# Seven products in every quad of gate and up, with two low parts a block made by an accumulating DMA

## The chip, the core and the metric

The kernel runs on one core of a Trainium2 chip. The metric is the time of one execution on the device in microseconds (us), lower is better. The engines that matter are TensorE (PE, with its weight loads as PEld), VectorE (DVE), ScalarE (ACT), GpSimd (POOL) and SyncE (SP, which issues the loads). Each works through its own list of instructions in a fixed order; semaphores let one wait for another.

## The reference

The block is a mixer (sparse attention beside a state-space branch), a SwiGLU channel mixer and a final norm, on 256 tokens with 2048 features, all in float32. The change touches the channel mixer:

```python
u2 = rms_norm(h, g_ffn[i])
gate, up = jnp.split(u2 @ w_ffn_in[i], 2, axis=-1)
h = h + (jax.nn.silu(gate) * up) @ w_ffn_out[i]
return rms_norm(h, g_final)
```

`w_ffn_in` is 2048 x 11264 (gate and up, 5632 each), `w_ffn_out` is 5632 x 2048.

## The kernel before

**Three matmuls a product.** TensorE multiplies a rounded format (float32r). Every float32 operand is split in a high part, `hi` (a rounding copy, by ACT), and a low part, `lo` = operand - `hi` (by DVE), and a product is hi x hi + hi x lo + lo x hi: three matmuls of 128 x 512. A weight block is 1 MB (128 x 2048), loaded by SP into a buffer `raw` (three of them, pool `wraw`). `hi` and `lo` are tiles of 128 x 1024; four pairs of them are in `whi`/`wlo` and every fifth pair comes from the pool `xtra` (`hl_tiles`, line 148), so five pairs are in flight.

**Gate and up.** The 11264 columns are taken as 11 pairs (`pair`, line 829) of 512 gate and 512 up columns. A pair goes through K = 2048 in four quads of 512, each of two blocks (`block7`, line 788), here called (quad, part): (0,0), (0,1), (1,0) ... (3,1). Tokens are two tiles of 128, columns two of 512, K slices two: a 2 x 2 x 2 product of matrices for the first block and the first half of the quad. Where `QUADS[q]` is 1, block (q,0) takes Strassen's seven products (Winograd's form) in place of eight, and needs sums of weight slices first: `ta` and `tb` (lines 747 to 749, three DVE instructions), and then hi and lo of seven 512-column operands in place of four. Block (q,1), and both blocks of a quad with 0, take the eight products of the common form. The sums go to seven banks of PSUM, `ps[1]` to `ps[7]`, over the whole pair. `QUADS = (1, 1, 1, 0)`: 3 x (7 + 8) + 16 = 61 products, 183 matmuls a pair.

After a pair come its closing steps: seven adds on DVE from PSUM (line 834), two Silu on ACT, two multiplications on DVE, eight transposes on PE (line 225) and their split in hi and lo, which gives the tile `act`.

**The order.** Nothing is ordered by hand; a list scheduler puts each engine's instructions in the order in which they would be ready, by priority. `tc.high_priority(PRE)` draws loads and splits ahead, and the closing adds have twice that.

**Down.** `gemm` (line 154) multiplies the `act` tiles of a group of pairs with `w_f2`, four column blocks `nb` of 512, and DVE adds each result into `h_sb` (line 869). There were two groups, pairs 0 to 4 and pairs 5 to 10 (`SPLIT_PAIRS = 5`). In the last group, `late=16` holds back the second token tile's last 16 K slices, so that the first tile's closing steps run beside them.

**Buffers.** The pool `big` has 11 tiles of 8 KB a partition. In gate and up it holds `h_sb` (2), `opa` (4, the operands of the quads), one `act` a pair and `gf`. The pool `smx` is closed before `xtra` is opened in its place.

Of the kernel before, what the change touches and what calls it, by code (L numbers as in the profile page):

```python
# [8 lines left out]
F32 = mybir.dt.float32  # L9
F32R = mybir.dt.float32r  # L10
# [4 lines left out]
P = 128  # L15
# [12 lines left out]
SH = 64  # L28
# [4 lines left out]
NEG_VIS = -3.0e38  # L33
NEG_SEL = -3.4028e38
NEG_BIAS = -1.0e30
SPLIT_PAIRS = 5

QUADS = (1, 1, 1, 0)


C_GM = 0
# [21 lines left out]
def hybrid_block(ctx, tc, xt, x, consts, cols, heads, gfin, w_a, w_i, w_m, w_g, w_ab, w_sb, w_o, w_f1, w_f2, out):  # L63
# [79 lines left out]
        return r  # L143

    xtra = []
    turn = [0]

    def hl_tiles():
        turn[0] += 1
# [114 lines left out]
    lhs_u = lhs_of(u_hi, u_lo)  # L264


    wz = cp.tile([P, 512], mybir.dt.bfloat16, name="wz")
    nc.vector.memset(wz, 0.0)
    for i in range(9):
        warm = sd_t([P, 512], name="warm")  # L270
# [30 lines left out]
    def rs(t):  # L301
        return rstd[:, t : t + 1]

    rope = cp.tile([P, 384], F32, name="rope")
    for t in range(T):
        for base, dst, w in ((K_CA, 0, 64), (K_SA, 128, 64), (K_CI, 256, 32), (K_SI, 320, 32)):
            nc.vector.tensor_scalar_mul(rope[:, dst + t * w : dst + (t + 1) * w], tabs[:, base - K_T + t * w : base - K_T + (t + 1) * w], rs(t))
# [18 lines left out]
        nc.vector.tensor_tensor(dv[:, :, 0, :], dv[:, :, 0, :], tv[:, :, 0, :], ALU.subtract)  # L326
        nc.vector.tensor_tensor(dv[:, :, 1, :], dv[:, :, 1, :], tv[:, :, 1, :], ALU.add)

    widx = cp.tile([P, T, NIDX], F32, name="widx")
    wk0 = mid_t([P, 1024], name="wk0")  # L330
    wk1 = mid_t([P, 1024], name="wk1")
    kdup = wk0[:, 0:256].rearrange("p (t n) -> p t n", t=T)
# [36 lines left out]
    tp = tr_t([P, 5, SH])  # L369
    for i, src in enumerate((r1[:, 0:P], r1[:, P:S], dl[:, 0:P], dl[:, P:S], rest)):  # L370
        nc.tensor.transpose(tp[:, i, :], src, ident[:SH, :SH])
    dcols = cp.tile([P, 5, SH], F32, name="dcols")
    nc.vector.tensor_copy(dcols, tp)


# [8 lines left out]
    kbd_l = mid_t([P, 2, S], F32R, name="kbdl")  # L384
    split(kbd_h, kbd_l, kbd)

    isc = [cp.tile([P, P * (t + 1)], F32, name=f"isc{t}") for t in range(T)]
    inits = [tabs[:, K_V0 - K_T : K_V0 - K_T + P], tabs[:, K_V1 - K_T : K_V1 - K_T + S]]
    seen = [False] * T

# [328 lines left out]

        return get  # L720

    def halves(raw, cuts):

        out = {}
        for i, n in cuts:
            hi, lo = (v[:, : n * 512] for v in hl_tiles())
            src = raw[:, i : i + n, :].rearrange("p k n -> p (k n)")
            nc.scalar.activation(hi, src, AF.Copy)  # L728
            nc.vector.tensor_tensor(lo, src, hi.bitcast(F32), ALU.subtract)  # L729
            for j in range(n):  # L730
                out[i + j] = hi[:, j * 512 : (j + 1) * 512], lo[:, j * 512 : (j + 1) * 512]
        return out

    nts = [0]

    def fetch(w, i, seven):

        with tc.high_priority(PRE):
            raw = wraw.tile([P, 4, 512], F32, tag="raw", name=nm("raw"))
            nc.sync.dma_start(raw.rearrange("p k n -> p (k n)"), w[i])  # L740
            if not seven:
                return halves(raw, ((0, 2), (2, 2)))
            b = halves(raw, ((0, 2),))
            nts[0] += 1
            ta = mid_t([P, 2, 512], name="ta")
            tb = mid_t([P, 2, 512], name="tb") if nts[0] % 2 else xtra[0].tile([P, 2, 512], F32, tag="tb", name=nm("tb"))
            nc.vector.tensor_tensor(ta, raw[:, 2:4, :], raw[:, 1:3, :], ALU.subtract)  # L747
            nc.vector.tensor_tensor(tb[:, 0, :], raw[:, 3, :], ta[:, 0, :], ALU.subtract)  # L748
            b["last"] = nc.vector.tensor_tensor(tb[:, 1, :], raw[:, 0, :], tb[:, 0, :], ALU.subtract)
            for base, t in ((6, tb), (4, ta)):  # L750
                for j, v in halves(t, ((0, 2),)).items():
                    b[base + j] = v
            b.update(halves(raw, ((3, 1),)))
            return b
# [7 lines left out]
    for nb in range(4):  # L762
        xr = ev_t([P, T, 512], "xr")
        for t in range(T):
            nc.gpsimd.dma_start(xr[:, t, :], x[t * P : (t + 1) * P, nb * 512 : (nb + 1) * 512])
        ps = gemm(w_o, 4 * nb, 512, KT, lhs_m)
        if nb == 3:
            ahead = fetch(w_f1, 0, QUADS[0])
        for t in range(T):
            a = h_sb[t][:, nb * 512 : (nb + 1) * 512]  # L770
            with tc.issue_after(ahead["last"].ins) if nb == 3 else nullcontext():
                nc.vector.tensor_tensor(a, ps[t], xr[:, t, :], ALU.add)
            nc.scalar.activation(xr[:, t, :], a, AF.Square, accum_out=sq4[:, t, nb : nb + 1])
        ops.append(quad_ops(nb))
# [6 lines left out]
    pctx.close()  # L781
    mm = ctx.enter_context(tc.tile_pool(name="mmf", bufs=7, space=bass.MemoryType.PSUM, reuse_waits="tile"))
    trp = ctx.enter_context(tc.tile_pool(name="trf", bufs=1, space=bass.MemoryType.PSUM, reuse_waits="tile"))
    gf = big_t([P, D], name="gf")
    sq5 = sm.tile([P, T, 5], F32, tag="sq5", bufs=1, name="sq5")
    acts = []

    def block7(w, first, quads, get, ahead=None):

        n7 = sum(quads)
        n1 = 4 * len(quads) - 2 * n7
        left = {i: 3 * n7 for i in (1, 6, 7)}
        left.update({i: 3 * (n7 + n1) for i in (2, 3, 4, 5)})
        ps = {}

        def prod(i, a, b):
            start = i not in ps
            if start:  # L800
                ps[i] = mm.tile([P, 512], F32, tag="mm", name=nm(f"p{i}"))
            for j, (x, y) in enumerate(((a[0], b[0]), (a[0], b[1]), (a[1], b[0]))):
                left[i] -= 1
                nc.tensor.matmul(ps[i], x, y, start=start and j == 0, stop=left[i] == 0)  # L804

        for q, seven in enumerate(quads):
            for part in range(2):
                if q == part == 0 and ahead is not None:
                    b = ahead
                else:  # L810
                    b = fetch(w, first + 2 * q + part, seven and part == 0)
                if seven and part == 0:
                    prod(1, get(q, 0), b[1])
                    prod(2, get(q, 2), b[0])
                    prod(6, get(q, 9), b[6])
                    prod(4, get(q, 3), b[7])
# [12 lines left out]
    def pair(p):  # L829
        ps = block7(w_f1, 8 * p, QUADS, lambda q, i: ops[q](i), ahead if p == 0 else None)  # L830
        xa, xb = ev_t([P, T, 512], "xa"), ev_t([P, T, 512], "xb")
        x1, x2, x3, x4 = xa[:, 0, :], xa[:, 1, :], xb[:, 0, :], xb[:, 1, :]
        r0, r1 = rstd2[:, 0:1], rstd2[:, 1:2]
        add = lambda o, i, b: nc.vector.tensor_tensor(o, ps[i], b, ALU.add)
        with tc.high_priority(2 * PRE):
            nc.scalar.activation(x1, ps[1], AF.Copy)
            add(x2, 6, x1)
            add(x3, 7, x2)
            add(x1, 2, x1)
            nc.scalar.activation(x1, x1, AF.Silu, scale=r0)  # L840
# [12 lines left out]
    for p0, p1 in ((0, SPLIT_PAIRS), (SPLIT_PAIRS, NPAIR)):
        acts = [pair(p) for p in range(p0, p1)]
        if p0 == 0:
            nc.gpsimd.dma_start(gf, gfin.partition_broadcast(P))
        else:
            hg = [big_t([P, D], name="hg") for _ in range(T)]
        lhs_a = lhs_quads(acts)
        for nb in range(4):  # L860
            ps = gemm(w_f2, first, 512, 4 * (p1 - p0), lhs_a, late=16 if p0 > 0 and nb == 3 else 0)
            first += p1 - p0
            last = p0 > 0 and nb == 3
            for t in range(T):
# [24 lines left out]
def _layout(inp):  # L889
# [56 lines left out]
    def pack7(n0, n1, quads):  # L946
# [32 lines left out]
```

## Time and profile before

| | before |
|---|---|
| median of 3 runs | 1976.47 us (1976.05 to 1976.49) |
| profiled execution | 1976.07 us |
| its span | 1974.1 us |
| gate and up, pairs 0 to 4 | 1256.6 to 1469.6 us |
| down, first group | 1469.6 to 1579.4 us |
| gate and up, pairs 5 to 10 | 1579.4 to 1833.3 us |
| down, second group, until the last matmul | 1833.3 to about 1965 us |
| loads, all queues | 375.7 MB, 190 GB/s |

Busy time says how much of the span an engine worked; whether it sets the time is read from what it waits for. Starts of neighbouring matmuls tell the pace of PE, since their durations overlap. A row of a group gives line, engine, operation, out<-in, its count, then busy time in us, mean ns of one, and the idle time of the engine before it with what ended it.

### The profile page before, as it was taken

Reading aid. Unit: us, or ns where it says so; the run is one execution under the profiler, and the core shown is the slowest. Engines: PE = TensorE matmul, PEld = TensorE weight load, DVE = VectorE, ACT = ScalarE, POOL = GpSimd, SP = SyncE. Lnnn points to the kernel's source line nnn. Section 1 sums busy time; section 2 is a strip of 40 time slices with the busy share of each in tenths; the row PEclk is TensorE's granted clock in tenths of the full one; section 3 lists DMA queues with packets and bytes.
Section 4 is the critical chain, followed back from the end, with each engine's and each line's share of the span. In section 5 each row is a group of like instructions: output and inputs, shape, how many; then the busy total and the mean of one; then the engine's idle time right before and its main releaser. Section 6 shows DMA issues by size and latency. Waiting matters only on the chain. (4 is left out here: it accounts for less than half of the span.)

```text
span 1974.1 us, 23523 instructions
## 1 busy us (share of the span) xinstructions
PE 1961.1 (99%) x9131; PEld 1626.0 (82%) x9131; DVE 1424.0 (72%) x1918; ACT 1040.2 (53%) x1249; POOL 36.2 (2%) x87
## 2 busy tenths in 40 slices
PE   9999999999999999999999999999999999999998
PEld 7898888888888888888888888788888888888886
DVE  7898867778778756566654556788975589888644
ACT  6575564654555544555554445655553355565443
POOL 0000000000000000000000000000000000000000
PEclk9999999999999999999999999999999999999999
DMA  7645555554554555544555556465565555556553
GB/s 279 229 153 183 184 200 178 192 194 169 204 202 157 185 184 182 189 171 163 190 181 192 192 184 203 164 212 197 179 226 192 192 193 210 194 199 222 188 196 113
DMA packets 54431, 375.70 MB, mean 190 GB/s; under 512 B 6304, under 2 KB 6816, under 8 KB 10672
## 3 DMA queue, kind: packets, MB, share of 16 engines
q1 hardware_dynamic: 51120, 360.86, 52.2%
q0 software_dynamic: 1968, 11.60, 1.7%
q8 instruction: 71, 1.16, 0.2%
q10 hardware_dynamic: 1232, 1.75, 0.2%
q14 instruction: 40, 0.33, 0.1%
HBM read 372.02 MB, written 2.16 MB: 190 GB/s over the span
## 5 line engine op out<-in xcount | busy, mean ns | idle before, releaser
L195 DVE TENSOR_TENSOR lo<-raw,hi 128x1024 fp32r<-128x1024 f32 (+2 forms) x513 | 619.1, 1209 | 394.2 <-ACT hi L194 392.3
L194 ACT ACTIVATE hi<-raw 128x1024 fp32r<-128x1024 f32 (+2 forms) x513 | 536.7, 1048 | 626.4 <-PE mm L165 555.5
L164 PE MATMUL mm<-lo,uh 128*128 128x512 f32 (+2 forms) x1184 | 461.0, 389 | 0.0
L165 PE MATMUL mm<-hi,ul 128*128 128x512 f32 (+2 forms) x1184 | 458.2, 388 | 0.2 <-DVE ul L216 0.2
L163 PE MATMUL mm<-hi,uh 128*128 128x512 f32 (+2 forms) x1184 | 453.0, 389 | 1.2 <-ACT hi L194 1.2
L804 PE MATMUL p<-hi,opa 128*128 128x512 f32 x924 | 308.2, 390 | 0.0
L163 PEld LDWEIGHTS mm<-hi,uh 128*128 128x128 f32 x1184 | 222.4, 188 | 44.9 <-ACT hi L194 2.1
L165 PEld LDWEIGHTS mm<-hi,ul 128*128 128x128 f32 x1184 | 222.6, 188 | 42.5 <-DVE ul L216 0.5
L164 PEld LDWEIGHTS mm<-lo,uh 128*128 128x128 f32 x1184 | 222.7, 188 | 41.1 <-issue 0.3
L728 ACT ACTIVATE hi<-raw 128x1024 fp32r<-128x1024 f32 (+1 forms) x176 | 169.6, 978 | 118.1 <-PE p L804 101.2
L729 DVE TENSOR_TENSOR lo<-raw,hi 128x1024 fp32r<-128x1024 f32 (+1 forms) x176 | 194.6, 1119 | 27.7 <-ACT hi L728 27.0
L804 PEld LDWEIGHTS p<-hi,opa 128*128 128x128 f32 x924 | 173.5, 188 | 36.0
L804 PE MATMUL p<-lo,opa 128*128 128x512 f32 x462 | 180.2, 390 | 0.4 <-DVE lo L729 0.4
L163 PE MATMUL mm<-hi,act 128*128 128x512 f32 x352 | 137.2, 390 | 0.0
L164 PE MATMUL mm<-lo,act 128*128 128x512 f32 x352 | 137.2, 390 | 0.0
L165 PE MATMUL mm<-hi,act 128*128 128x512 f32 x352 | 137.0, 389 | 0.0
L804 PE MATMUL p<-hi,opb 128*128 128x512 f32 x352 | 130.5, 392 | 0.8 <-ACT opf L693 0.8
L804 PEld LDWEIGHTS p<-lo,opa 128*128 128x128 f32 x462 | 86.8, 188 | 18.6 <-DVE lo L729 0.9
L165 PE MATMUL mm<-hi,yl 128*128 128x512 f32 x256 | 100.4, 392 | 0.0
L164 PE MATMUL mm<-lo,yh 128*128 128x512 f32 x256 | 100.4, 392 | 0.0
L163 PE MATMUL mm<-hi,yh 128*128 128x512 f32 x256 | 100.2, 395 | 0.0
L804 PEld LDWEIGHTS p<-hi,opb 128*128 128x128 f32 x352 | 66.1, 188 | 14.5 <-ACT opf L693 1.3
(260 smaller groups left out, 2314.3 us busy)
## 6 DMA issues: line engine op xcount, KB each, us to landing
raw<-in_w_f_dram SPq DMA_DIRECT2D x132, 1024.0 KB, 4.8
raw<-in_w_m_dram SPq DMA_DIRECT2D x104, 1024.0 KB, 4.8
raw<-in_w_sb_dram SPq DMA_DIRECT2D x32, 1024.0 KB, 4.8
raw<-in_w_g_dram SPq DMA_DIRECT2D x32, 1024.0 KB, 4.8
raw<-in_w_ab_dram SPq DMA_DIRECT2D x16, 1024.0 KB, 4.8
raw<-in_w_o_dram SPq DMA_DIRECT2D x16, 1024.0 KB, 4.8
abc<-acum_d POOLq DMA_DIRECT2D x8, 1024.0 KB, 5.2
raw<-in_w_i_dram SPq DMA_DIRECT2D x8, 768.0 KB, 4.4
```

The costliest lines, as they stand in the source:

```text
L163: nc.tensor.matmul(o, lh, rh, start=(kt == 0), stop=False)
L164: nc.tensor.matmul(o, lh, rl, start=False, stop=False)
L165: nc.tensor.matmul(o, ll, rh, start=False, stop=(kt == nk - 1))
L194: hi_ops.append(nc.scalar.activation(hi[:, o], src[:, o], AF.Copy))
L195: nc.vector.tensor_tensor(lo[:, o], src[:, o], hi[:, o].bitcast(F32), ALU.subtract)
L728: nc.scalar.activation(hi, src, AF.Copy)
L729: nc.vector.tensor_tensor(lo, src, hi.bitcast(F32), ALU.subtract)
L804: nc.tensor.matmul(ps[i], x, y, start=start and j == 0, stop=left[i] == 0)
```

## The change

- `QUADS = (1, 1, 1, 1)`: quad 3 takes seven products too. A pair is 60 products, 180 matmuls. `w_f1` is packed to match, on the host.
- In pairs 1 to 10 block (0,1) is fetched ahead, in the middle of the pair before (`early`, called when block (3,0) has been fetched). Its two low parts are not made by DVE: ACT writes `lo` = -`hi` (a copy with scale -1), POOL issues a DMA that adds `raw` to `lo` in SBUF (512 KB each, two a block), and ACT writes `hi`. These tiles, `dhi` and `dlo`, come from `big`.
- A fourth buffer `raw`, in `xtra`, for every fourth fetch: these are the blocks (1,1) and the (0,1) that are made by DMA. Small tiles move from `cp` to `smx` and `mid` to make room.
- The down projection runs in four groups, pairs 0-1, 2-4, 5-7 and 8-10, so that at most three `act` tiles are held; `gf` is loaded at the last group. `h` is added to 32 times in place of 16. `late` is 12, all K slices of the last group.

```diff
-SPLIT_PAIRS = 5
-
-QUADS = (1, 1, 1, 0)
+PAIR_GROUPS = ((0, 2), (2, 5), (5, 8), (8, 11))
+
+QUADS = (1, 1, 1, 1)
...
-    wz = cp.tile([P, 512], mybir.dt.bfloat16, name="wz")
+    wz = mid_t([P, 512], mybir.dt.bfloat16, name="wz")
...
-    rope = cp.tile([P, 384], F32, name="rope")
+    rope = smx.tile([P, 384], F32, tag="rope", bufs=1, name="rope")
...
-    def halves(raw, cuts):
+    def halves(raw, cuts, by_dma=False):
+
 
         out = {}
-        for i, n in cuts:
-            hi, lo = (v[:, : n * 512] for v in hl_tiles())
+        if by_dma:
+            his, los = big_t([P, 2, 1024], F32R, name="dhi"), big_t([P, 2, 1024], F32R, name="dlo")
+        for c, (i, n) in enumerate(cuts):
             src = raw[:, i : i + n, :].rearrange("p k n -> p (k n)")
-            nc.scalar.activation(hi, src, AF.Copy)
-            nc.vector.tensor_tensor(lo, src, hi.bitcast(F32), ALU.subtract)
+            if by_dma:
+                hi, lo = his[:, c, :], los[:, c, :]
+                nc.scalar.activation(lo, src, AF.Copy, scale=-1.0)
+                nc.gpsimd.dma_start(lo, src, accum_op=ALU.add)
+                nc.scalar.activation(hi, src, AF.Copy)
+            else:
+                hi, lo = (v[:, : n * 512] for v in hl_tiles())
+                nc.scalar.activation(hi, src, AF.Copy)
+                nc.vector.tensor_tensor(lo, src, hi.bitcast(F32), ALU.subtract)
...
-    def fetch(w, i, seven):
+    ahead = {}
+
+    def fetch(w, i, seven, by_dma=False):
 
         with tc.high_priority(PRE):
-            raw = wraw.tile([P, 4, 512], F32, tag="raw", name=nm("raw"))
+            turn[1] += 1
+            raw = (xtra[0] if turn[1] % 4 == 0 else wraw).tile([P, 4, 512], F32, tag="raw", name=nm("raw"))
             nc.sync.dma_start(raw.rearrange("p k n -> p (k n)"), w[i])
             if not seven:
-                return halves(raw, ((0, 2), (2, 2)))
+                return halves(raw, ((0, 2), (2, 2)), by_dma)
...
-                if q == part == 0 and ahead is not None:
-                    b = ahead
-                else:
-                    b = fetch(w, first + 2 * q + part, seven and part == 0)
+                b = ahead.pop((q, part), None) or fetch(w, first + 2 * q + part, seven and part == 0)
+                if q == len(quads) - 1 and part == 0:
+                    early()
...
+        def early():
+            if p + 1 < NPAIR:
+                ahead[0, 1] = fetch(w_f1, 8 * p + 9, False, True)
...
-    for p0, p1 in ((0, SPLIT_PAIRS), (SPLIT_PAIRS, NPAIR)):
+    for p0, p1 in PAIR_GROUPS:
+        end = p1 == NPAIR
         acts = [pair(p) for p in range(p0, p1)]
...
-            ps = gemm(w_f2, first, 512, 4 * (p1 - p0), lhs_a, late=16 if p0 > 0 and nb == 3 else 0)
+            ps = gemm(w_f2, first, 512, 4 * (p1 - p0), lhs_a, late=12 if end and nb == 3 else 0)
```

**Where instructions move, first place: the loads at the border of two pairs, on SP.** Before, at the border of pairs 2 and 3, the loads stand in the order of their blocks: (2,1), (3,0), (3,1) of pair 2, then (0,0), (0,1), (1,0) of pair 3.

```order
L740 DMA raw_10875<-in_w_f_dram 128x2048
L740 DMA raw_10909<-in_w_f_dram 128x2048
L740 DMA raw_10943<-in_w_f_dram 128x2048
L740 DMA raw_11006<-in_w_f_dram 128x2048
L740 DMA raw_11057<-in_w_f_dram 128x2048
L740 DMA raw_11091<-in_w_f_dram 128x2048
```

Now, on SP at the border of pairs 3 and 4: (2,1), (3,0), then (0,1) of the next pair (11593), (3,1), then (1,1) of the next pair (11806), and only then (0,0) (11687) and (1,0) (11762).

```order
L751 DMA raw_11536<-in_w_f_dram 128x2048
L751 DMA raw_11570<-in_w_f_dram 128x2048
L751 DMA raw_11593<-in_w_f_dram 128x2048
L751 DMA raw_11624<-in_w_f_dram 128x2048
L751 DMA raw_11806<-in_w_f_dram 128x2048
L751 DMA raw_11687<-in_w_f_dram 128x2048
L751 DMA raw_11762<-in_w_f_dram 128x2048
```

What moved: 11593 and 11806 share the fourth buffer, so 11806 waits until both accumulating DMAs have read 11593, and (0,0) of the next pair stands behind it. Three of the six borders inside groups have this order; at the other three (0,0) stands ahead of that load. On ACT, in the same place, the negations (`dlo`) stand between the hi of blocks (2,0) (11492), (2,1) and (3,0):

```order
L737 ACTIVATE hi_11511<-raw_11492 128x512
L732 ACTIVATE dlo_11596<-raw_11593 128x1024
L734 ACTIVATE dhi_11595<-raw_11593 128x1024
L737 ACTIVATE hi_11538<-raw_11536 128x1024
L732 ACTIVATE dlo_11596<-raw_11593 128x1024
L734 ACTIVATE dhi_11595<-raw_11593 128x1024
L212 ACTIVATE act_11324<-tr_11332 128x512
L737 ACTIVATE hi_11572<-raw_11570 128x1024
```

The second negation stands right behind the hi of the first tile of (2,1); before, nothing stood there but the hi of the next tiles.

**Second place: PE where the first group of pairs ends and its down projection begins.** Before (after pair 4, `act_10653` is the tile of pair 1, `act_11667`, not yet here, that of pair 4), the transposes of the last pair stand among matmuls of earlier pairs, 63 of which follow before the first that reads `act_11667`:

```order
L163 MATMUL mm_11684<-hi_11721,act_10653 128x512
L225 MATMUL tr_11668<-kc,xa_11653 128x128
L225 MATMUL tr_11668<-kc,xb_11654 128x128
L225 MATMUL tr_11668<-kc,xa_11653 128x128
L225 MATMUL tr_11668<-kc,xb_11654 128x128
L164 MATMUL mm_11684<-lo_11722,act_10653 128x512
L165 MATMUL mm_11684<-hi_11721,act_10653 128x512
```

Now (after pair 1, `act_10340` is the tile of pair 0 and `act_10688` that of pair 1) all matmuls on pair 0 for two column blocks, 48 of them, come first, and the first matmul on `act_10688` stands right behind the four transposes that it is made from:

```order
L165 MATMUL mm_10776<-hi_10795,act_10340 128x512
L225 MATMUL tr_10689<-kc,xa_10674 128x128
L225 MATMUL tr_10689<-kc,xb_10675 128x128
L225 MATMUL tr_10689<-kc,xa_10674 128x128
L225 MATMUL tr_10689<-kc,xb_10675 128x128
L163 MATMUL mm_10703<-hi_10741,act_10688 128x512
L164 MATMUL mm_10703<-lo_10742,act_10688 128x512
L163 MATMUL mm_10704<-hi_10741,act_10688 128x512
```

At the other three such places 22 or more matmuls stand between.

More of the change, by code (lines that the diff above doesn't have):

```diff
@@ L145, in hybrid_block @@
     xtra = []
-    turn = [0]
+    turn = [0, 0]
     def hl_tiles():
@@ L327, in rope_apply @@
         nc.vector.tensor_tensor(dv[:, :, 1, :], dv[:, :, 1, :], tv[:, :, 1, :], ALU.add)
-    widx = cp.tile([P, T, NIDX], F32, name="widx")
+    widx = smx.tile([P, T, NIDX], F32, tag="widx", bufs=1, name="widx")
     wk0 = mid_t([P, 1024], name="wk0")
@@ L371, in hybrid_block @@
         nc.tensor.transpose(tp[:, i, :], src, ident[:SH, :SH])
-    dcols = cp.tile([P, 5, SH], F32, name="dcols")
+    dcols = smx.tile([P, 5, SH], F32, tag="dcols", bufs=1, name="dcols")
     nc.vector.tensor_copy(dcols, tp)
@@ L385, in hybrid_block @@
     split(kbd_h, kbd_l, kbd)
-    isc = [cp.tile([P, P * (t + 1)], F32, name=f"isc{t}") for t in range(T)]
+    isc = [smx.tile([P, P * (t + 1)], F32, tag=f"isc{t}", bufs=1, name=f"isc{t}") for t in range(T)]
     inits = [tabs[:, K_V0 - K_T : K_V0 - K_T + P], tabs[:, K_V1 - K_T : K_V1 - K_T + S]]
@@ L767, in hybrid_block @@
         if nb == 3:
-            ahead = fetch(w_f1, 0, QUADS[0])
+            ahead[0, 0] = fetch(w_f1, 0, QUADS[0])
         for t in range(T):
             a = h_sb[t][:, nb * 512 : (nb + 1) * 512]
-            with tc.issue_after(ahead["last"].ins) if nb == 3 else nullcontext():
+            with tc.issue_after(ahead[0, 0]["last"].ins) if nb == 3 else nullcontext():
                 nc.vector.tensor_tensor(a, ps[t], xr[:, t, :], ALU.add)
@@ L783, in hybrid_block, with block7 @@
     trp = ctx.enter_context(tc.tile_pool(name="trf", bufs=1, space=bass.MemoryType.PSUM, reuse_waits="tile"))
-    gf = big_t([P, D], name="gf")
     sq5 = sm.tile([P, T, 5], F32, tag="sq5", bufs=1, name="sq5")
     acts = []
-    def block7(w, first, quads, get, ahead=None):
+    def block7(w, first, quads, get, ahead, early):
         n7 = sum(quads)
@@ L829, in pair @@
     def pair(p):
-        ps = block7(w_f1, 8 * p, QUADS, lambda q, i: ops[q](i), ahead if p == 0 else None)
+        def early():
+            if p + 1 < NPAIR:
+                ahead[0, 1] = fetch(w_f1, 8 * p + 9, False, True)
+        ps = block7(w_f1, 8 * p, QUADS, lambda q, i: ops[q](i), ahead, early)
         xa, xb = ev_t([P, T, 512], "xa"), ev_t([P, T, 512], "xb")
@@ L852, in hybrid_block @@
     first = 0
-    for p0, p1 in ((0, SPLIT_PAIRS), (SPLIT_PAIRS, NPAIR)):
+    for p0, p1 in PAIR_GROUPS:
+        end = p1 == NPAIR
         acts = [pair(p) for p in range(p0, p1)]
-        if p0 == 0:
+        if end:
+            gf = big_t([P, D], name="gf")
             nc.gpsimd.dma_start(gf, gfin.partition_broadcast(P))
-        else:
             hg = [big_t([P, D], name="hg") for _ in range(T)]
@@ L860, in hybrid_block @@
         for nb in range(4):
-            ps = gemm(w_f2, first, 512, 4 * (p1 - p0), lhs_a, late=16 if p0 > 0 and nb == 3 else 0)
+            ps = gemm(w_f2, first, 512, 4 * (p1 - p0), lhs_a, late=12 if end and nb == 3 else 0)
             first += p1 - p0
-            last = p0 > 0 and nb == 3
+            last = end and nb == 3
             for t in range(T):
@@ L869, in hybrid_block @@
                     nc.vector.tensor_tensor(a, ps[t][:, c * n : (c + 1) * n], a, ALU.add)
-                    if p0 > 0:
+                    if end:
                         jk = ev_t([P, 1024], "jk")[:, :n]
@@ L956, in _layout @@
         pack7(wf1[:, 512 * p : 512 * (p + 1)], wf1[:, DFF + 512 * p : DFF + 512 * (p + 1)], QUADS) for p in range(NPAIR)])
-    cut = SPLIT_PAIRS * 512
-    a["w_f2"] = np.concatenate([pack(wf2, (s, s + 512), k0, k1) for k0, k1 in ((0, cut), (cut, DFF)) for s in range(0, D, 512)])
+    a["w_f2"] = np.concatenate([pack(wf2, (s, s + 512), 512 * p0, 512 * p1) for p0, p1 in PAIR_GROUPS for s in range(0, D, 512)])
     return a
```

## The prediction, made before the changed kernel ran

> **What bounds the kernel now.** First the engine totals of the page, then what PE waits for in the whole run.
>
> ```profile
> PE 1961.1 (99%) x9131; PEld 1626.0 (82%) x9131; DVE 1424.0 (72%) x1918; ACT 1040.2 (53%) x1249; POOL 36.2 (2%) x87
> ...
> PE p L804 <- ACT opf L693: 0.8, 1, 0.8
> PE p L804 <- DVE lo L729: 0.4, 1, 0.4
> ```
>
> PE is busy for 99% of the span, and the channel mixer's two rows in its list of waits come to 1.2 us. So nothing that other engines save can help there, and a matmul that goes shortens the run by its pace, as long as no new wait opens. The pace comes from the timeline of PE in gate and up (start, duration): the first two and the last of 24 matmuls in a row.
>
> ```profile
> 1650.70 0.39 PE L804 MATMUL p<-hi,opb 128*128 128x512 f32 x1
> 1650.93 0.39 PE L804 MATMUL p<-lo,opa 128*128 128x512 f32 x1
> ...
> 1655.91 0.39 PE L804 MATMUL p<-hi,opa 128*128 128x512 f32 x1
> ```
>
> 23 steps in 5.21 us are 0.2265 us a matmul; the 0.39 is a pipelined duration and not the cost. Next, how near the other engines are, by stretches: one whole pair, and the sum of three (columns: stretch, length, then busy us of PE, PEld, DVE, ACT, POOL, granted clock, DMA share, GB/s); then the opening of gate and up, and the first down projection.
>
> ```profile
> 1658.84:1701.32 42.48, 42.48 (x192) 35.14 (x191) 36.98 (x43) 24.31 (x28) 0.00 (x0) 1.00 0.58 198
> ...
> sum 127.42, PE 127.42 PEld 105.41 DVE 112.27 ACT 72.83 POOL 0.00; mean PE 42.47 PEld 35.14 DVE 37.42 ACT 24.28 POOL 0.00
> ...
> 1256.60:1469.60 213.00, 211.72 (x948) 174.58 (x947) 184.73 (x206) 123.79 (x143) 2.08 (x6) 1.00 0.57 199
> 1469.60:1579.40 109.80, 109.80 (x489) 90.89 (x489) 61.67 (x60) 43.84 (x43) 0.61 (x1) 1.00 0.55 195
> ```
>
> A pair takes 42.47 us, all of it PE; DVE works for 37.42 (88%) and ACT for 24.28. In down DVE is at 56%. The granted clock is 1.00 throughout, so it is no term here. DVE is the engine that could take PE's place.
>
> **The change part by part.** *Removed on PE.* 61 products become 60, three matmuls a pair, 33 in all: 33 x 0.2265 = **7.5 us**. All of it is on the path, since PE waits for nothing. A pair is then 42.47 - 0.68 = 41.8 us.
>
> *DVE in gate and up.* Its cost is read from starts, which follow each other back to back:
>
> ```profile
> 1638.72 1.22 DVE L729 TENSOR_TENSOR lo<-tb,hi 128x1024 fp32r<-128x1024 f32 x1
> 1639.86 1.22 DVE L729 TENSOR_TENSOR lo<-ta,hi 128x1024 fp32r<-128x1024 f32 x1
> 1640.99 0.69 DVE L729 TENSOR_TENSOR lo<-raw,hi 128x512 fp32r<-128x512 f32 x1
> 1641.59 0.68 DVE L213 TENSOR_TENSOR act<-tr,act 128x512 fp32r<-128x512 f32 x1
> ```
>
> 1.13 us for 1024 elements, 0.60 for 512. A block of seven products costs ta 1.13, tb 2 x 0.60 and low parts 3 x 1.13 + 0.60 = 6.3 us, a common one 2 x 1.13 = 2.3. So quad 3 adds 4.1, and the block made by DMA takes 2.3 away: +1.8 us, 39.2 of 41.8 us. ACT gains about 1.6 for quad 3 and two negations, 4 us, to 28 of 41.8. Both stay under PE, which hides them. The cover that is left on DVE is 2.6 us a pair where 5.05 stand now; if it is gone, each us over costs a us in each of 11 pairs. I take 0, and keep what that could be as a rival.
>
> *The opening.* Quad 3's operands need more work on DVE just where PE already waited for it (0.4 us above).
>
> ```profile
> L696 DVE TENSOR_TENSOR opf<-opf x13: 284/291/693, 1193.9 to 1259.0; 128x128 f32<-128x128 f32 x9, 128x256 f32<-128x256 f32 x3, 128x512 f32<-128x512 f32 x1
> L213 DVE TENSOR_TENSOR opx<-opf,opx x3: 284/285/285, 1198.1 to 1244.8; 128x128 fp32r<-128x128 f32 x3
> ```
>
> One of 0.69 goes; four of 0.29, one of about 0.4 and an opx of 0.29 come: +1.2 us, once. Bounds 0 and 1.2; I take 0.6.
>
> *Four groups.* Down has the same matmuls. `h` is added to 16 times more, 0.60 each: 10 us of DVE, beside a PE that leaves it 44% free; nothing. At the first border of pairs and down, the order puts a matmul right behind the transposes of its own operand, so PE sits through the last transpose and ACT's split:
>
> ```profile
> L225 PE MATMUL tr<-kc,xa 128*128 128x128 f32 x44 | 10.7, 271 | 0.0
> L212 ACT ACTIVATE act<-tr 128x512 fp32r<-128x512 f32 x22 | 13.1, 595 | 7.5 <-PE tr L225 7.1
> ```
>
> 0.27 + 0.60 = 0.9 us, once, taken in full. Elsewhere 23 or more matmuls (5.2 us) cover it. Bounds 0.9 and, if all four borders showed it, 3.6. `late` 12 leaves 36 matmuls, 8.2 us, beside the first tile's closing steps, which are adds, squares and scalings of some 6 us in the tail; nothing.
>
> *The accumulating DMAs and the loads behind them.* No accumulating DMA is in the trace. The nearest rows (line, count, size, median us from issue to landing):
>
> ```profile
> raw<-in_w_f_dram SPq DMA_DIRECT2D x132, 1024.0 KB, 4.8
> ...
> abc<-acum_d POOLq DMA_DIRECT2D x8, 1024.0 KB, 5.2
> ...
> xr<-in_x_dram POOLq DMA_DIRECT2D x8, 256.0 KB, 3.9
> xt<-in_xt_dram SPq DMA_DIRECT2D x3, 512.0 KB, 8.2
> ```
>
> From below 3.9 us (less data, same queue), from above 8.2 (the same 512 KB where the queues were full). I take 5.2: the same queue, and 1 MB is what the sum has to read (512 KB of `raw` and 512 KB of `lo`). Call it D. PE itself has time: the block is used after the end of the pair. The loads have less. Let 0 be the end of a pair on PE. ACT makes the second negation after the hi of the first tile of (2,1), whose buffer held the last tile of (1,1), five tiles earlier; PE is done with that one 21 + 24 + 21 + 24 = 90 matmuls, 20.4 us, before 0. With that hi and the negation (1.0 each by the page's group of hi, below), POOL issues at -18.3, and the sum lands at -18.3 + D.
>
> ```profile
> L728 ACT ACTIVATE hi<-raw 128x1024 fp32r<-128x1024 f32 (+1 forms) x176 | 169.6, 978 | 118.1 <-PE p L804 101.2
> ```
>
> Only then does SP issue the load of the next (1,1), and behind it that of (0,0), which takes 4.8 us and between 0 and 4.8 more for the one ahead; in the middle, 7.2. DVE wants (0,0) early enough for ta, lo, half of tb and the next ta (4.0 us) ahead of the closing add that waits for `ps[2]`, complete 7 matmuls (1.6 us) before 0: at -5.6. So D has 18.3 - 7.2 - 5.6 = 5.5 us, and each us over costs a us at three borders. At 5.2 it costs 0, at 8.2 8 us. Queued behind the waiting load are all later weights, since SP issues everything in order; POOL has nothing else queued until `gf`. The DMAs add 10 x 1 MB to 376, to engines at a share of 0.58.
>
> *Sum*, against the profiled execution: 1976.07 - 7.5 + 0.6 + 0.9 = 1970.1. The median stood 0.4 above that execution: **1970.5 us**.
>
> **A rule that speaks against it.** In the rows POOL's issues took 547 and 594 ns while DVE was at work:
>
> ```profile
> L479 POOL DMA_DIRECT2D abc<-acum_d x8 | 4.7, 594 | 210.7 <-DVE E L502 207.4 <-DMA acum_d<-wk 3.3
> L765 POOL DMA_DIRECT2D xr<-in_x_dram x8 | 4.4, 547 | 470.2 <-ACT qT L583 232.2 <-ACT xr L773 224.4 <-DVE acc L655 13.6
> ```
>
> The Trainium skill, page "SBUF — State Buffer", section "SBUF: two separate sides", warns that DMAs from GpSimd have their descriptors written by it through a port that it shares with DVE, so that a DVE operation in a two-port mode shuts it out, and names 620 ns that became 3100. By that rule an issue would take up to 2.5 us more; the trace does not agree so far, but neither row stands in gate and up.
>
> **The rivals.**
> *The load behind the sum (slower).* Place: SP, three borders. Price: 3 x (D - 5.5). For it: my slack is worked out to some 2 us, DMAs in gate and up share engines at 0.58 with loads, and a DMA that adds may run slower than a copy. Against: the order's other three borders have no such wait, and D near 5.2 costs nothing. It eats the gain of 6.0 at D = 7.5; at the upper row, 8.2, 1978.6; at 10, 1984.
> *Partly eaten.* D between 6.5 and 7.5, or up to 0.5 us at each inner border for the DVE, which there has no gap from -5.6 on: 3 to 6 us back, 1973.5 to 1976.5.
> *POOL shut out.* An issue that waits for a DVE operation of 1.2 us makes D 6.4: 2.7 us, 1973.2. Nothing in the rows shows it.
> *DVE becomes the bound (slower).* If its idle time of 5.05 us a pair stays (it is waits for loads and free tiles), a pair takes 39.2 + 5.05 = 44.3, 2.5 over PE: 11 x 2.5 = 27, 1998. It decides from 2.6 us of idle on. Against: those waits come where DVE is ahead, and the fourth buffer lets loads run further ahead.
> *The change doesn't do what it says* can't be for the matmuls: 33 fewer stand in the order.
>
> **How the numbers follow.** Forecast, 1969 to 1972.5: 0.50. Partly eaten and POOL shut out, 1972.5 to 1976.5: 0.25. The load behind the sum past its point, up to 1980: 0.10, beyond: 0.08. DVE as the bound: 0.07. The lower end is the full 7.5, with part of the 1.2 us of waits: 1968.5. The upper end takes D at 8.2 with 1 us beside it: 1979.5; left out are 0.15 above and 0.03 below. About 0.2% (4 us) is what a measurement can tell from no change: faster, under 1972.5, 0.53; the same, up to 1980.4, 0.32; slower 0.15.
>
> **What would show it.** 180 matmuls a pair, 41.8 us between the same rows of two pairs inside a group, DVE at 39 busy in it; a wait of PE of about 1 us on ACT's `act` at the first down projection; accumulating DMAs that land within 5.5 us, and no wait of PE for `lo`, `hi` or `dlo` at borders inside a group. Wrong would be: SP waiting on a DMA of POOL's at every second such border, with DVE's `ta` waiting for the load behind and PE for `lo`; or PE waits in every pair.

## The result and the profile after

The changed kernel takes **2003.9 us** at the median (1999.3 to 2007.0, four runs) against 1976.5 (1976.05 to 1976.99): a ratio of **1.0137** (95% interval 1.0122 to 1.0152). It is slower, where 1970.5 was forecast. Not only the median moved: runs of the kernel before lie within 1 us, those of the changed one within 8.

The engine totals of the page, and what PE waited for in the whole run:

```profile
PE 1970.8 (98%) x9098; PEld 1620.3 (81%) x9098; DVE 1457.1 (73%) x1974; ACT 1071.6 (53%) x1292; POOL 55.2 (3%) x107
...
PE p L814 <- ACT hi L737: 6.6, 10, 1.3
PE p L814 <- DVE lo L738: 4.9, 10, 1.4
PE mm L164 <- DVE lo L195: 4.6, 3, 2.1
PE mm L163 <- ACT hi L194: 1.6, 3, 1.0
PE av L643 <- ACT pT L212: 1.3, 1, 1.3
PE mm L163 <- ACT act L212: 1.2, 1, 1.2
```

33 matmuls fewer, and yet PE is "busy" for 9.7 us more, since busy time hides waits: a row of 0.39 us outlasts the step of 0.2265 and so covers the start of a wait, and a row is 0.50 us long behind a wait and 0.63 at half the clock. So the totals do not say where the time is; the starts of PE's matmuls do. Summed over the 11 pairs from a pair's first matmul to the next instruction of another stage, and over what lies between (transposes and down projections):

| us of the profiled executions | before | after | difference | forecast |
|---|---|---|---|---|
| start of the first transposes of `h` | 1191.7 | 1198.4 | +6.7 | 0 |
| gate and up, 11 pairs | 460.8 | 475.7 | +14.9 | -7.5 + 0.6 |
| transposes and down | 247.5 | 255.4 | +7.9 | +0.9 |
| span | 1974.1 | 2003.8 | +29.7 | -6.0 |

The 7.5 us came off where nothing waits. Pair 2, from its first matmul to that of pair 3 (all such stretches begin and end 0.2 to 0.3 us early; stretch, length, busy us of PE, PEld, DVE, ACT, POOL, clock, DMA share, GB/s), has 41.0 us with its transposes moved behind it:

```profile
1403.30:1444.30 41.00, 41.00 (x181) 33.70 (x181) 28.89 (x30) 25.24 (x27) 1.71 (x2) 1.00 0.68 222
1444.30:1487.20 42.90, 42.66 (x189) 34.44 (x189) 36.52 (x43) 24.57 (x28) 1.71 (x2) 1.00 0.62 204
1487.20:1532.00 44.80, 42.63 (x186) 33.67 (x185) 40.26 (x46) 28.14 (x32) 1.72 (x2) 1.00 0.58 187
```

Pairs 3 and 4 do not keep that pace. So gate and up got 22.3 us of new waits (14.87 + 7.47), down 7.9 and the mixer, which the diff hardly touches, 6.7.

**The sums.** The DMA issues by line (count, KB, median us from issue to landing), and what SP waited for:

```profile
raw<-in_w_f_dram SPq DMA_DIRECT2D x132, 1024.0 KB, 4.9
...
dlo<-raw POOLq DMA_DIRECT2D x20, 512.0 KB, 7.0
...
SPq L751 <- DMA dlo<-raw: 67.9, 12, 10.5
```

7.0 us in place of 5.2, and SP waits for them in 12 places, up to 10.5 us. At the border of pairs 3 and 4 the two sums took 8.0 and 7.7 us, and the load of (0,0) landed 1.9 us ahead of its pair, where it did 12 us ahead in the kernel before. DVE, which has done the old pair's low parts by then, waits with `ta`, and PE waits 4.7 us into the new pair for a `hi` that is made from these sums of weights (DVE's rows ahead of and behind the wait, and PE's longest wait):

```profile
1482.33 0.68 DVE L847 TENSOR_TENSOR xb<-p,xa 128x512 f32<-128x512 f32 x1
1485.61 1.23 DVE L758 TENSOR_TENSOR ta<-raw 128x1024 f32<-128x1024 f32 x1 [2.60 <-DMA raw<-in_w_f_dram]
...
1492.11 0.50 PE L814 MATMUL p<-hi,opb 128*128 128x512 f32 x1 [1.01 <-ACT hi L737]
```

**The border of pairs 0 and 1**, DVE's rows and the one of PE that waits:

```profile
1296.94 0.68 DVE L738 TENSOR_TENSOR lo<-raw,hi 128x512 fp32r<-128x512 f32 x1
1301.98 1.23 DVE L758 TENSOR_TENSOR ta<-raw 128x1024 f32<-128x1024 f32 x1 [4.35 <-DMA raw<-in_w_f_dram]
1303.12 1.22 DVE L738 TENSOR_TENSOR lo<-raw,hi 128x1024 fp32r<-128x1024 f32 x1
...
1304.39 0.50 PE L814 MATMUL p<-lo,opa 128*128 128x512 f32 x1 [1.36 <-DVE lo L738]
```

DVE stands still for 4.35 us because `ta` of the next pair waits for the load of (0,0). The `lo` behind it is that of block (3,1) of the *old* pair, and PE stops for it, 20 matmuls ahead of the pair's end. At this border, what is queued behind the waiting instruction is what costs. `ta` stands ahead of an old pair's last low parts at the borders into pairs 1, 3, 6 and 9, and behind them at those into 4, 7 and 10.

**The mixer.** At 990 us, in the product with the gate weights, stands what was not there before (engine, line, operation):

```profile
989.50 1.05 ACT L194 ACTIVATE hi<-raw 128x1024 fp32r<-128x1024 f32 x1
...
990.24 0.68 DVE L619 SCALAR_TENSOR_TENSOR sc<-lg,isc 128x512 f32<-128x512 f32 x1
...
990.96 1.22 DVE L624 TENSOR_REDUCE mx<-sc 128x4 f32<-128x1024 f32 x1
...
992.09 1.22 DVE L195 TENSOR_TENSOR lo<-raw,hi 128x1024 fp32r<-128x1024 f32 x1
...
993.36 0.79 PE L164 MATMUL mm<-lo,uh 128*128 128x512 f32 x1 [2.03 <-DVE lo L195]
```

This `lo` stands behind the last reading of `isc` (L619). `isc` is one of the small tiles that moved to the pool `smx`, and the fifth `hi`/`lo` pair lies in `xtra`, which takes that pool's place.

### The profile page after: what moved, and what is told of

Its sections match the earlier page's. It is cut to its first block, busy times and chain, and to the rows that moved or that the text cites. A ratio compares the mean times of both kernels' runs of the same rounds, so it can differ in the third digit from the quotient of the medians.

```text
span 2003.8 us, 23587 instructions
## 1 busy us (share of the span) xinstructions
PE 1970.8 (98%) x9098; PEld 1620.3 (81%) x9098; DVE 1457.1 (73%) x1974; ACT 1071.6 (53%) x1292; POOL 55.2 (3%) x107
## 4 chain that ended last, share of the span: by engine, by line
PE 81%; DVE 8%; DMA 7%; issue 2%; ACT 1%; POOL 0%; SPq 0%; POOLq 0%; DVEq 0%; ACTq 0%
PE mm L164 23%; PE mm L163 23%; PE mm L165 23%; PE p L814 7%; DMA raw<-in_w_f_dram 6%; DVE lo L738 4%; DMA dlo<-raw 1%; PE yp L514 1%; DVE ta L758 1%; DVE xa L847 1%; ACT hi L737 1%; DVE tb L759 1%; DVE xb L847 1%; PE tr L428 1%; PE tr L225 0%
## 5 line engine op out<-in xcount | busy, mean ns | idle before, releaser
L814 PE MATMUL p<-hi,opa 128*128 128x512 f32 x760 | 260.0, 392 | 3.7 <-ACT hi L737 3.5
L165 PEld LDWEIGHTS mm<-hi,ul 128*128 128x128 f32 x1184 | 223.3, 189 | 42.3 <-DVE ul L216 0.3
L737 ACT ACTIVATE hi<-raw 128x1024 fp32r<-128x1024 f32 (+1 forms) x156 | 143.2, 934 | 124.2 <-PE p L814 71.6
L738 DVE TENSOR_TENSOR lo<-raw,hi 128x1024 fp32r<-128x1024 f32 (+1 forms) x156 | 164.4, 1069 | 39.2 <-ACT hi L737 39.1
L814 PEld LDWEIGHTS p<-hi,opa 128*128 128x128 f32 x760 | 142.6, 188 | 36.5 <-ACT hi L737 7.1
L814 PE MATMUL p<-lo,opa 128*128 128x512 f32 x380 | 150.2, 395 | 3.3 <-DVE lo L738 2.7
L814 PE MATMUL p<-hi,opb 128*128 128x512 f32 x312 | 117.6, 392 | 3.9 <-ACT hi L737 3.0
L814 PEld LDWEIGHTS p<-lo,opa 128*128 128x128 f32 x380 | 71.3, 188 | 23.5 <-DVE lo L738 9.2
L164 PEld LDWEIGHTS mm<-lo,act 128*128 128x128 f32 x352 | 66.5, 189 | 17.2 <-DVE lo L195 3.2
```

The costliest lines, as they stand in the source:

```text
L164: nc.tensor.matmul(o, lh, rl, start=False, stop=False)
L165: nc.tensor.matmul(o, ll, rh, start=False, stop=(kt == nk - 1))
```

## The experiments

Times are medians; the kernel before had 1976.4 to 1976.8 us beside them.

**1. One load held.** On the changed kernel, the load of block (1,1) of pair 0 kept in its place:

```diff
-            nc.sync.dma_start(raw..., w[i])
+            with tc.issue_after(ahead["load"]) if turn[1] == 4 else nullcontext():
+                ahead["load"] = nc.sync.dma_start(raw..., w[i]).ins
```

> Only the load of the fourth fetch, block (1,1) of pair 0, is kept behind the load before it on SP; in the changed kernel it stood in the mixer, between two loads of gate weights, 272 us before its pair. Question: what made the first transposes of h start 6.7 us later (1198.4 against 1191.7). Theory load: the early load takes DMA time and a place on SP there; then the 6.7 us come back, 1997 us. Theory tile: the hi and lo tiles that the mixer takes from the pool xtra now lie where isc lay and wait for its last reading; then nothing changes, 2003 to 2004 us, with the wait of 2 us for lo at about 993 us still there.

2006.0 us (2002.6 to 2006.2); the transposes of `h` began at 1198.5. The early load is not it.

**2. No tile of `xtra` in the mixer.**

```diff
-        if xtra and turn[0] % 5 == 0:
+        if xtra and turn[0] % 5 == 0 and turn[1]:
```

> The mixer takes every hi and lo from the four buffers of whi and wlo and none from xtra until gate and up begins; the early load stays where it is. Theory tile: the stall of 6.4 us at 987 to 996 us goes, gate and up begins 6.5 us earlier, 1997 us. Theory load: no change, 2003 to 2004 us. If the mixer needs its fifth pair of buffers, new small waits in the last products of the mixer take some of it back.

1999.1 us. The start of PE's transposes is back at 1191.8 (duration, first and last start):

```profile
L690 PE MATMUL tr<-kc,h x32: 270/272/331, 1191.8 to 1256.6; 128*128 128x128 f32 x32
```

The 6.7 us of the start are the place of these tiles; the median fell by 4.8. Some 1.6 of the 6.7 are matmuls at half the clock behind the wait of 2.03 us (last section): in run 3, with the same wait and the clock kept, the transposes began at 1196.8. That it is `isc` below them, and not another small tile, is argued from the rows above and was not tried alone.

**3. All loads in program order** (the edit of 1 with `turn[1] > 1`).

> Every load of gate and up is issued in the order in which the program names it, so none stands behind a load that waits for an accumulating DMA except the next one that needs that buffer. Theory A (SP's wait behind the sum): the stalls of 3.8 us at the starts of pairs 4, 7 and 10 go (11.4 us), and so does the wait for lo at the first down projection with the slow matmuls behind it (4 us): 1988 to 1989 us, with (0,0) loaded 13 to 16 us before its pair again. Theory B (the sums take DMA time from the loads, whoever stands first): (0,0) still lands late, the stalls stay, 2000 us or more.

2001.3 us, 2.6 less. The wait for `lo` at the first down projection went (that stage took 46.7 us in place of 51.1), but gate and up took 478.9 us against 475.7: the stalls at pairs 4, 7 and 10 stayed, though SP no longer held the load of (0,0) behind a sum. It was issued 12 us ahead of its pair in place of 8.7 and landed 5 us ahead, 6 to 8 us later, beside other loads and the sums. So the place in SP's queue is not the whole price: without it the loads come late beside the sums.

**4. The low parts by DVE**, no negation and no sum:

```diff
-                nc.scalar.activation(lo, src, AF.Copy, scale=-1.0)
-                nc.gpsimd.dma_start(lo, src, accum_op=ALU.add)
                 nc.scalar.activation(hi, src, AF.Copy)
+                nc.vector.tensor_tensor(lo, src, hi.bitcast(F32), ALU.subtract)
```

> The low parts of the early block are made by DVE as raw - hi, in the same tiles; the negations and the accumulating DMAs are gone, all else is as changed. DVE then has about 41.5 of 41.6 us in a pair. Theory A (all stalls of gate and up come from the sums: SP behind them, ACT's negations ahead of hi, slower loads): gate and up loses its 22 us of stalls but for 2 to 4 at the opening, 1980 to 1984 us. Theory C (DVE is the bound): its waits of some 3 to 5 us a pair are paid by PE in each of 11 pairs, 2025 us or more.

1984.6 us. What the change made to relieve DVE cost 19 us.

**5. A copy in the place of the sum** (`accum_op` left out). The instructions of all engines stand in the same order as in the changed kernel.

> The DMAs of the early block copy raw over lo in place of adding to it (so its low parts are wrong); negations, waits and order stay. The sum took 7.0 us from issue to landing (median), 4.5 at best, and a load of 1 MB takes 4.8. Theory adding: adding is slow in itself; a copy lands in 3.9 to 5 us, SP waits less, and 8 to 12 us come back: 1992 to 1996 us. Theory traffic: the time is the queueing beside the loads, so a copy takes 6 to 7 us too, and nothing changes: 2001 to 2006 us.

1986.4 us, 17.5 less, more than expected. The DMAs of this run; then the same queue in the changed kernel and in the one before (packets, MB, share of the 16 DMA engines):

```profile
dlo<-raw POOLq DMA_DIRECT2D x20, 512.0 KB, 5.4
q0 software_dynamic: 4848, 22.09, 3.2%
```

```profile
q0 software_dynamic: 4848, 22.09, 4.3%
```

```profile
q0 software_dynamic: 1968, 11.60, 1.7%
```

20 sums took 4.3% of 2003.8 us less 1.7% of 1974.1, which is 52.6 us of all engines, 2.6 each; 20 copies of the same bytes (3.2% of 1982.9) 1.5 each. Adding is what is dear, and the loads beside it pay: the load of (0,0) of pairs 1 and 9 took 8.3 and 7.3 us beside the sums, 4.8 and 4.9 beside the copies.

**6. Negations without DMA, and 7. DMA without negations.** In 6 DVE writes the low parts over ACT's negations, in 7 a DMA copies `raw` into `lo` and ACT writes only `hi`.

> ACT still writes the negations of the early block in front of its other copies, but DVE then writes the low parts over them as raw - hi, and no DMA adds. With DVE alone and no negation it was 1984.6 us, with sums 2003.9. Theory ACT: two more copies of 1 us that wait for the load stand ahead of hi of (2,1); then most of the 19 us stays, 1996 us or more. Theory DMA: the 19 us are the sums and what waits for them; 1984 to 1987 us.

> The early block's lo is filled by a plain DMA copy of raw (its low parts are wrong), with no negation on ACT; POOL's DMAs wait for the load alone. The counterpart of the run with negations and no DMA. Theory ACT: 1985 to 1990 us. Theory DMA: the transfers slow the loads and hold SP all the same, 1996 us or more; the two runs' losses against 1984.6 should add up to about 19 us if nothing else is in it.

1995.3 and 1988.2 us: 10.7 and 3.6 above run 4. In run 6 the negations cost 10.7; there DVE makes the low parts, and ACT copies the early block twice ahead of `hi` of (2,1). But runs 5 and 7, where a DMA writes `lo`, differ in nothing but the negations and the order that follows from them, and the one that has them is not slower (1986.4 against 1988.2). So a price of the negations in the changed kernel is not shown. The two don't add to 19.3; 7 copies where the change adds.

**8. The seven products alone**, on the kernel before: `QUADS = (1, 1, 1, 1)` and nothing else.

> The kernel before with seven products in all four quads and nothing else: no early block, no DMA sums, three raw buffers, two groups. DVE then has 41.5 of a pair's 41.8 us. Theory slack: loads and buffers run far enough ahead, and the 33 matmuls come off but for 1 us at the opening: 1969 to 1971 us. Theory DVE: its waits for loads and free tiles are no longer covered and cost 1 to 3 us at each of the 9 inner borders: 1979 us or more.

1985.2 us, ratio 1.0045 (1.003 to 1.006). One pair of it:

```profile
1668.30:1711.30 43.00, 42.08 (x189) 34.49 (x188) 40.62 (x48) 23.98 (x28) 0.00 (x0) 1.00 0.56 196
```

DVE is busy for 40.6 us, and the pair takes 43.0 where PE needs 41.8. Gate and up took 469.0 us against 460.8: 15.6 us of waits for 7.5 saved.

**9. The low parts by POOL**, with both repairs (2 and 3), and **12. the same idea on the kernel before with its seven products**, for four low parts a pair:

```diff
-                nc.scalar.activation(lo, src, AF.Copy, scale=-1.0)
-                nc.gpsimd.dma_start(lo, src, accum_op=ALU.add)
                 nc.scalar.activation(hi, src, AF.Copy)
+                nc.gpsimd.tensor_tensor(lo, src, hi.bitcast(F32), ALU.subtract)
```

```diff
-            nc.vector.tensor_tensor(lo, src, hi.bitcast(F32), ALU.subtract)
+            (nc.gpsimd if i == 2 else nc.vector).tensor_tensor(lo, src, hi.bitcast(F32), ALU.subtract)
```

> The low parts of the early block are made by a subtraction on POOL (no negation, no DMA), and both repairs are in: the mixer takes nothing from xtra, and the loads of gate and up are issued in program order. DVE has the 39.2 us a pair of the forecast. Theory DVE (what stayed when DVE made these low parts was DVE's own load): 1971 to 1974 us. Theory late block (POOL's subtraction is slow, or it slows DVE beside it, or ACT's copies ahead of hi are what costs): 1979 us or more. No row of POOL on tiles of this size exists, so its duration is open.

> The kernel before with seven products in all quads and the second low part of each plain block (four a pair in gate and up, all such blocks of its pairs) made by a subtraction on POOL in place of DVE. DVE then has 41.5 - 4.5 = 37.0 us of 41.8 in a pair, as before the change. Theory DVE: the stalls of 16 us of the run with the quads alone go: 1969 to 1972 us. Theory late: POOL's subtraction takes over 3 us and the tiles come late, or it slows DVE: 1980 us or more.

1991.1 and 2008.7 us: both worse than leaving the work to DVE. Rows of DVE and POOL in run 12:

```profile
1700.82 0.68 DVE L213 TENSOR_TENSOR act<-tr,act 128x512 fp32r<-128x512 f32 x1
1701.42 2.28 DVE L749 TENSOR_TENSOR tb<-raw,tb 128x512 f32<-128x512 f32 x1
...
1710.24 0.68 DVE L213 TENSOR_TENSOR act<-tr,act 128x512 fp32r<-128x512 f32 x1
1710.84 2.29 DVE L748 TENSOR_TENSOR tb<-raw,ta 128x512 f32<-128x512 f32 x1
...
1699.17 3.97 POOL L729 TENSOR_TENSOR lo<-raw,hi 128x1024 fp32r<-128x1024 f32 x1 [10.56 <-ACT hi L728]
1710.16 2.43 POOL L729 TENSOR_TENSOR lo<-raw,hi 128x1024 fp32r<-128x1024 f32 x1 [7.01 <-ACT hi L728]
```

A subtraction of 0.68 us on DVE takes 2.28 while POOL works: it ends about 0.6 us behind POOL's. Of what POOL takes over, DVE spends a good part standing.

**10. Both repairs, sums kept.**

> The changed kernel with both repairs (nothing from xtra in the mixer, loads in program order), the sums kept. If the parts add, 2003.9 - 4.8 - 2.6: 1996 to 1997 us, with the stalls of 2 to 6 us at the six inner borders still there. If the early load in the mixer or SP's place hid more than they showed alone: 1990 us or less.

1992.5 us, 4 less than the parts added to.

**11. Quad 3 plain in the changed kernel**, `QUADS = (1, 1, 1, 0)`, to see if the sums hurt only because DVE is nearly full.

> The changed kernel with eight products in quad 3 again: 33 matmuls more (7.5 us), DVE 4.1 us less in each pair, sums, buffers and groups as changed. Theory late loads alone (a load that lands 5 us late stops PE whatever DVE has to do): 2008 to 2012 us. Theory DVE tight (late loads cost because DVE has no room to catch up): most of the 22 us of stalls in gate and up go, and 1986 to 1992 us are left, of which 6.5 are the mixer's and 4 the first down projection's.

2008.4 us: the stalls stayed, with 4.1 us of DVE's work a pair less. Gate and up took 483.7 us, 22.9 more than before with as many matmuls (some 7 of them in two stretches of 6.8 us at half the clock). The sums cost by themselves.

**13. `ta` behind the old pair's low parts**, on run 10; **15. the same without sums**; **14. both repairs, low parts by DVE**; **16. one sum of the two**, on 13 (the first low part is DVE's). `ahead["lo"]` is the last `lo` that DVE was given before, here that of (3,1):

```diff
+            old = ahead.get("lo")
...
+            with tc.issue_after(old) if i and i % 8 == 0 else nullcontext():
-            nc.vector.tensor_tensor(ta, raw[:, 2:4, :], raw[:, 1:3, :], ALU.subtract)
+                nc.vector.tensor_tensor(ta, raw[:, 2:4, :], raw[:, 1:3, :], ALU.subtract)
```

> Both repairs as in the run before (1992.5 us), and DVE's ta of the next pair's block (0,0) is kept behind the low parts of (3,1) of the old pair. Theory place (DVE waits with ta for a late load, and the old pair's low parts stand behind it): the stalls ahead of a pair's end go, 4 to 8 us come back, 1985 to 1988 us. Theory load (PE waits for (0,0)'s own low parts a little later anyway): 1991 to 1994 us.

> Both repairs, and the early block's low parts by DVE (no sums). If the mixer's 6.5 us add to the run with DVE's low parts alone (1984.6): 1977 to 1979 us. If SP's order matters there too, 1 us less; if DVE is the bound in every pair, 1980 us or more.

> As the run before it, with ta kept behind the low parts of (3,1). Theory place: its stalls of about 1 us at the six inner borders go, 1973 to 1975 us, faster than the kernel before the change. Theory DVE (41.5 us of work in a pair of 41.6 leaves nothing to move): no difference to the run before it, within 1 us.

> As the run with sums, both repairs and ta behind, but only the second low part of the early block is a sum; the first is made by DVE. DVE has 40.3 us in a pair, the DMA engines one sum in place of two. If a sum's price is its own traffic and wait, the time lies halfway between that run and the one with none (ta behind in both). If the two sums hurt because one queues behind the other, it is near the run with none, or below it.

13: 1987.9, 4.6 less than run 10. 15: 1981.1, but 14: **1973.6** (ratio 0.9987, 0.9978 to 0.9996), so there the same edit loses 7.5. In these four runs `ta` had better wait behind where the loads are late, and had better not where they are in time. 16: 1977.7, below both 13 and 15. Run 14 is the only one that beats the kernel before. A pair of it, from its first matmul to the next pair's:

```profile
1429.80:1471.60 41.80, 41.80 (x189) 34.52 (x189) 41.00 (x47) 25.67 (x29) 0.00 (x0) 1.00 0.58 214
```

This is the 41.8 us of the forecast, at a DVE that is busy for 41.0 of them.

**17. One sum, order left free**, and **18. run 14 with quad 3 plain.**

> Both repairs, one of the early block's two low parts by a sum, the other by DVE, DVE's order left free. Two sums gave 1992.5 us, none 1973.6. Theory traffic: each sum costs the loads and SP the same, halfway, about 1983 us. Theory queue: the harm is the second sum that lands 1 to 3 us behind the first; 1974 to 1977 us. Theory DVE: relief of 1.1 us a pair is worth more than one sum costs; 1973 us or less.

> The version with both repairs and no sums (1973.6 us), with quad 3 taking eight products again: 33 matmuls more, DVE back at 37.4 us a pair. If PE is bound in every pair and buffers and groups bring nothing: 1977 to 1978 us (the kernel before and 1 us for the first down projection), so that of the 7.5 us the seven products keep 3.5 to 4.5. If the early block costs time in itself, 1980 us or more; if it gains by itself, under 1976.

1977.0 and 1977.4 us. The first sum, its negation and what it takes from DVE come to 3.4 us over none, the second to 15.5 more (1992.5). And the seven products of quad 3 bring 3.8 us in run 14, while early block, fourth buffer and groups bring nothing by themselves (ratio 1.0005, 0.9997 to 1.0014).

## Why the prediction was wrong

**Held.** The matmul's price: 41.8 us in run 14's pair 3, as worked out (42.0 and 42.3 in pairs 9 and 6, which another pair follows too). The wait for ACT's `act` at the first down projection: 0.9 forecast, 1.2 in the list of waits. POOL's issues were not shut out: 0.86 us a sum by the trace, 0.53 a copy. And, in size, the deadline of -5.6 for (0,0) at the three borders on which it was worked out.

**"I take 5.2"** for the sum's D, from a plain DMA on the same queue, is the step that failed: it was 7.0 at the median and 7.7 to 8.0 at the border of pairs 3 and 4. The bounds, 3.9 to 8.2, held that; the choice in them did not. A sum is not a copy: 2.6 us of all DMA engines in place of 1.5. Run 5 prices this at 17.5 us with nothing else changed. The issue at "-18.3" was off as well: the second sum was issued at -16.9. From its landing to that of (0,0) it took 7.2 us, as forecast. So (0,0) landed at -1.9 in place of -5.9.

Landing of (0,0), from issues and landings of the trace, and the pair's time over its best, 40.8 us, in two runs whose engines have the same order:

| pair | changed: landing, over 40.8 | run 5: landing, over 40.8 |
|---|---|---|
| 4 | -1.9, 4.0 | -4.7, 1.3 |
| 7 | -1.9, 4.0 | -3.8, 2.1 |
| 10 | -1.9, 4.0 | -4.7, 1.3 |
| 1 | -7.1, 2.6 | -9.0, 0.7 |
| 9 | -7.1, 2.5 | -9.0, 0.7 |
| 3 | -8.3, 1.4 | -8.7, 1.1 |
| 6 | -8.9, 0.7 | -9.0, 0.6 |

In the kernel before, too, a pair inside a group takes 0.3 us more than one that begins a group (41.77 against 41.48), with the load at -12. Less this 0.3, pairs 4, 7 and 10 lost a us for each us behind -5.6, as the prediction said each us over would: 11 us at three borders. What PE waited for at pair 4, by its list of waits, was `hi` and `lo` (2.2 us) and not a closing add; the size fits, the path does not. (At pairs 4 and 10 of run 5 DVE came to `ta` 0.2 us behind the landing, so there the load is not the only bound.)

**The other borders at nothing.** Seven borders lie inside groups, where the prediction counted six and priced three. At the other four (into pairs 1, 3, 6 and 9) `ta` stands ahead of the old pair's last low parts, which PE reads 20 matmuls (4.7 us) before the pair's end. With the 2.4 us from the landing to PE's matmul at pair 1, a load behind -7.1 stops PE in the old pair, and from the landing on DVE has no gap: its rows follow back to back from 1301.98 to 1320. Less the same 0.3, these four pairs lost a us for each us behind some -9.4, 6.0 in all, and the old pair ahead of pair 1 took 2.2 us more than in run 5. The -9.4 is read off the table and not worked out. In other orders the landing alone does not tell the loss: -4.5 cost 6.2 at pair 7 of run 3, -8.4 cost 0.4 at pair 4 of run 17.

The rival "the load behind the sum" had the right sign, the right transfer and three of the right places. That SP's order is all of it is refuted by run 3: in program order the load lands late too.

**DVE at "0"** is not shown to have failed in the changed kernel: run 11 takes 4.1 us of DVE's work from each pair, and the waits stayed. As a way to cost DVE it did fail in run 8. The rival was set to decide at 2.6 us of idle time in a pair; run 8 has 2.4 (43.0 - 40.6, a DVE that is 95% busy), and gate and up lost 15.6 us. Its loads of (0,0) are issued later (13.9 to 16 us ahead of an inner pair, where the kernel before had 16.3 to 16.8), but run 14's no earlier (13.3 to 15.4), and run 14's gate and up (456.0) lost 2.6 of the 7.5 us with DVE busy for 41.0 of 41.8 in pair 3. So what run 8 lacks, among run 14's buffer, early block and groups, stays open.

**No term at all** for the mixer, 6.7 us. The diff moves `isc` from one pool to another; the forecast read this as room made and not as a new neighbour in memory, whose last reader a later tile has to wait for. The order of the changed kernel showed it: PE's rows differ from 985 us on.

**ACT's negations**, taken as hidden at 4 us "to 28 of 41.8", cost 10.7 in run 6 and nothing in run 5 against 7: open for the changed kernel.

**Down**: of the 7.9 us, 6.0 went in run 3 (249.4 us), 4.5 of them at the first projection, where the down weights stood behind a load that waited for a sum and some 1.8 were matmuls at half the clock. The other 1.9, where 0.9 was forecast, are in run 14 as well, without sums, and so belong to the four groups.

Not settled: why the second sum costs over four times the first, and why the place of `ta` helps with late loads and hurts without. Both suggest that at a DVE this full a kernel's time hangs on its order as much as on its work.

## What to carry to other kernels

Work that is taken from a full engine and given to DMA has to be priced on the DMA engines too, and at the place where loads are already in flight; an adding DMA is not priced by a copy's row. Where a load's slack is worked out, every border needs its own deadline: that of the load's consumer, and that of what stands behind this consumer on its engine. And a small tile that moves to another pool is an edit to every stage that uses the memory next.

## What the runs showed of the hardware

**A short wait can halve PE's pace.** At the first down projection PE waited for 2.1 us, and the next matmuls start 0.43 us apart; the granted clock in that stretch is 0.62:

```profile
1361.80 0.65 PE L164 MATMUL mm<-lo,act 128*128 128x512 f32 x1 [2.13 <-DVE lo L195]
...
1362.24 0.63 PE L165 MATMUL mm<-hi,act 128*128 128x512 f32 x1
...
1362.67 0.63 PE L164 MATMUL mm<-lo,act 128*128 128x512 f32 x1
...
1361.00:1365.00 4.00, 3.20 (x8) 2.55 (x9) 3.68 (x4) 0.00 (x0) 0.00 (x0) 0.62 0.81 287
```

Some nine matmuls at 0.20 us more add about 1.8 us to a wait of 2.1. No length of the wait decides it in these runs. The wait of 2.03 us in the mixer halved the clock in the changed kernel and in runs 1, 4, 5, 6 and 7, and not in runs 3 and 11. Single waits of up to 1.6 us left the pace as it was, but in run 3 waits of 0.2, 1.0 and 0.9 us within 4 us did the same as the one here. In run 2 a wait of 2.45 us, and in run 12 one of 3.44, did nothing; run 12, with the granted clock behind it:

```profile
1779.20 0.50 PE L804 MATMUL p<-hi,opa 128*128 128x512 f32 x1 [3.44 <-DVE xa L834]
1779.55 0.40 PE L804 MATMUL p<-lo,opa 128*128 128x512 f32 x1
...
1779.00:1783.00 4.00, 3.54 (x14) 2.52 (x15) 4.00 (x7) 2.29 (x3) 0.00 (x0) 1.00 0.60 246
```

The Trainium skill, page "TensorE: Matmul & The Clock Gate", Part 1, has the clock halved after at least one idle window of about 3.4 us; here 2.1 us did it, behind two matmuls and a gap of 0.2, and 3.44 us did not.

**POOL and DVE exclude each other, for some forms.** In run 12's rows DVE's `act<-tr,act` keeps its 0.68 us beside POOL, and `tb<-raw,ta` does not. The Trainium skill, page "SBUF — State Buffer", section "SBUF: two separate sides", says that a DVE operation with two inputs in SBUF is locked out by a GpSimd operation that reads SBUF, for its whole length; `tr` lies in PSUM, and the rows agree. Of the trap with DMAs from GpSimd, on the same page, no run showed anything: issues took 0.53 to 0.96 us. DVE's rows beside the sums' issues were all TENSOR_TENSOR; other operations were not tried.
